# A QKV projection kernel whose first two row pairs are scheduled anew: half of the early x loads on GpSimd's queue, weight casts between evacuations, block sums in order of first use

## The chip, the cores and the metric

One core of one Trainium2 chip. The metric is the device time of one execution in microseconds (us); the profile is that of one execution, and its span leaves out a little that the time holds.

## The reference

```
def reference(x, w_qkv):              # x: 16 x 512 x 768, w_qkv: 768 x 2304, float32
    qkv = np.matmul(x, w_qkv)
    hidden = x.shape[-1]
    q, k, v = qkv[..., :hidden], qkv[..., hidden:2*hidden], qkv[..., 2*hidden:]
    return np.stack([q, k, v], axis=0).astype(np.float32)
```

So it is one product of 8192 x 768 by 768 x 2304, its result cut into three.

## The kernel before, in words

The 8192 rows of x are taken as 32 pairs of 128 rows (p = 0 to 31, `NP` is 32). The 2304 columns of the weights are two groups of 1024 (q = 0 and 1), each of two blocks of 512 (c = 0 and 1), and a remainder of 256 columns.

**A pair's way in.** `load_x` (L110) brings the 256 x 768 values into `xin` by four DMAs of 192 KB, two on SP's queue and two on ScalarE's. `transpose` (L118) is one VectorE instruction in 32 x 32 blocks, `xf<-xin`. `round_x` (L126) casts to bfloat16 on GpSimd, `xb<-xf`, and `sums_x` (L130) makes on GpSimd five blocks `s` out of `xf` (L136 to L140). `xin` has 3 buffers, `xf` 2, `xb` 4, `s` 2.

**Pairs 2 to 31** are computed by `two` (L236), with a scheme of seven half-depth products for each 256 x 1024 group (`product` and `do`, L154 and L173) on weights that were combined beforehand: `b1` (block c = 0 in bfloat16), `b22` (a rounded copy of the lower half of block c = 1) and four sums `t` (`sum_w`, L96, VectorE), which for q = 0 lie in `t_0` and for q = 1 in `t_1`. `t_1` takes the buffers of the staged q = 0 blocks (tag `tq`), so it can be written only when these have been read for the last time. Inside `two`, after the first product of each group, `early` transposes, casts and sums pair p + 1 and loads pair p + 2. The remainder (`rem`, L213) is 12 matmuls of 256 columns for each pair. A pair's first group uses q = 0 and its second q = 1.

**Pairs 0 and 1** are computed by plain matmuls (`direct`, L225: two row blocks of six matmuls of 512 columns, each evacuated on ScalarE at L234), since that needs only the weights as they arrive. The order of all this is written out by hand (L261 to L326); every engine runs its own instructions in that order and waits at the first that isn't ready. Weights land in stages: `str` (the remainder), `st` 108 and 110 (q = 0, blocks 0 and 1, 1536 KB each) and `st` 119, 121, 123, 125 (q = 1: halves h = 0 and 1 of block 0, then of block 1, 768 KB each), all on SP's queue, in between the loads of x. Block 0 of q = 0 is cast to `b1` on VectorE, the other three on ScalarE: `b1` of q = 1, and for c = 1 a buffer `bt` of which there is one.

Two places in this order are touched most. On ScalarE both casts of the next block (L280) stand behind all four evacuations of the block before. And `load_x(3)` stands at L322, behind the stores of pairs 0 and 1 on SP's queue and behind everything else on ScalarE's.

Of the kernel before, what the change touches and what calls it, by code (L numbers as in the profile page):

```python
# [9 lines left out]
def kernel(  # L10
# [20 lines left out]
    nc = tc.nc  # L31
    P = 128
    G = 32
# [4 lines left out]
    KT = K // P  # L38
# [3 lines left out]
    CB = 512  # L42
# [5 lines left out]
    bf16 = mybir.dt.bfloat16  # L48
    ident = mybir.ActivationFunctionType.Identity
# [10 lines left out]
    bt_pool = ctx.enter_context(tc.tile_pool(name="bt", bufs=1))  # L60
# [10 lines left out]
    b1 = [w_pool.tile([P, KT, CB], bf16, name=f"b1_{q}") for q in range(2)]  # L71
    b22 = [w_pool.tile([P, KH, CB], f32r, name=f"b22_{q}") for q in range(2)]
# [6 lines left out]
    def load_w(dst, j0, nj, off, cols):  # L79
        rows = w_qkv.rearrange("(p j) n -> p j n", j=KT)  # L80
        nc.sync.dma_start(dst[:], rows[:, j0:j0 + nj, off:off + cols])

    stage = {}

    def load_blocks(q, c):
        if q == 0:
            t = tq_pool.tile([P, KT, CB], fp32, name="st0", tag="tq")
            load_w(t, 0, KT, Q_OFF[q] + c * CB, CB)
            stage[q, 0, c], stage[q, 1, c] = t[:, :KH, :], t[:, KH:, :]
        else:  # L90
            for h in range(2):
                t = big_pool.tile([P, KH, CB], fp32, name="st1", tag="big")
                load_w(t, h * KH, KH, Q_OFF[q] + c * CB, CB)
                stage[q, h, c] = t[:]

    def sum_w(q, n):  # L96
        t1, t2, t3, t4 = ts[q]
        o, in0, in1 = {
            1: (t1, stage[q, 0, 1], stage[q, 0, 0]),
            2: (t2, stage[q, 1, 1], t1),  # L100
            3: (t3, stage[q, 1, 1], stage[q, 0, 1]),
            4: (t4, stage[q, 1, 0], t2),
        }[n]
        nc.vector.tensor_tensor(o, in0, in1, op=sub)

    xin, xf, xb, sr = {}, {}, {}, {}

    def load_x(p):  # L110
        t = xin_pool.tile([P, 2 * P // G, KC], fp32, name="xin")
        rows = x_flat[p * 2 * P:(p + 1) * 2 * P, :].rearrange("(g b) k -> b g k", b=G)
        for i in (0, 2, 1, 3):
            eng = nc.sync if i < 2 else nc.scalar
            eng.dma_start(t[i * G:(i + 1) * G], rows[:, :, i * KC:(i + 1) * KC])  # L115
        xin[p] = t

    def transpose(p):  # L118
        t = xf_pool.tile([P, KT, 2 * P], fp32, name="xf")
        nc.vector.transpose(  # L120
            t.rearrange("p j (g b) -> p g j b", b=G),
            xin.pop(p).rearrange("p g (a j) -> p g j a", a=G),
        )
        xf[p] = t

    def round_x(p):  # L126
        xb[p] = xb_pool.tile([P, KT, 2 * P], bf16, name="xb")
        nc.gpsimd.tensor_copy(out=xb[p][:], in_=xf[p][:])  # L128

    def sums_x(p):  # L130
        t = xf.pop(p)
        a11, a12 = t[:, :KH, :P], t[:, KH:, :P]
        a21, a22 = t[:, :KH, P:], t[:, KH:, P:]
        s = s_pool.tile([P, 5, KH, P], f32r, name="s")
        g = nc.gpsimd
        g.tensor_tensor(s[:, 1], a21, a22, op=add)  # L136
        g.tensor_tensor(s[:, 2], s[:, 1], a11, op=sub)  # L137
        g.tensor_tensor(s[:, 3], a11, a21, op=sub)  # L138
        g.tensor_copy(out=s[:, 0], in_=a22)  # L139
        g.tensor_tensor(s[:, 4], a12, s[:, 2], op=sub)  # L140
        sr[p] = s
# [28 lines left out]
    def bank():  # L170
        return ps_pool.tile([P, CB], fp32, name="ps")
# [41 lines left out]
    def rem(p):  # L213
        ps = ps_pool.tile([P, 2, REM], fp32, name="ps")
        for r in range(2):
            for j in range(KT):
                nc.tensor.matmul(  # L217
                    ps[:, r, :], xb[p][:, j, r * P:(r + 1) * P], w_rem[:, j, :],
                    start=(j == 0), stop=(j == KT - 1), skip_group_check=True,
                )  # L220
        o = or_pool.tile([P, 2, REM], fp32, name="orem")
        nc.scalar.activation(o[:], ps[:], ident)  # L222
        nc.sync.dma_start(rows_of(1, p, R_OFF - H, R_OFF - H + REM), o[:])

    def direct(p, c, o, w):  # L225

        for r in range(2):
            ps = bank()
            for j in range(KT):
                nc.tensor.matmul(  # L230
                    ps[:], xb[p][:, j, r * P:(r + 1) * P], w[:, j, :],
                    start=(j == 0), stop=(j == KT - 1),
                )
            nc.scalar.activation(o[:, r, c * CB:(c + 1) * CB], ps[:], ident)  # L234
# [24 lines left out]


    load_x(0)  # L261
    tiny = w_pool.tile([P, 1], fp32, name="tiny")
    nc.vector.memset(tiny[:], 0.0)
    nc.scalar.activation(tiny[:], tiny[:], ident)
    st_rem = big_pool.tile([P, KT, REM], fp32, name="str", tag="big")
    load_w(st_rem, 0, KT, R_OFF, REM)
    load_x(1)
    load_blocks(0, 0)
    load_blocks(0, 1)
    load_x(2)  # L270
    o0 = [quad(p, 0) for p in range(2)]
    load_blocks(1, 0)
    load_blocks(1, 1)
    o1 = [quad(p, 1) for p in range(2)]

    def cast(q, h, c, w, eng):

        dst = w[:, h * KH:(h + 1) * KH, :]
        if eng is nc.scalar:
            eng.activation(dst, stage[q, h, c], ident)  # L280
        else:
            eng.tensor_copy(out=dst, in_=stage[q, h, c])

    transpose(0)
# [8 lines left out]
    direct(0, 0, o0[0].o, b1[0])  # L293
    direct(1, 0, o0[1].o, b1[0])
    bt = bt_pool.tile([P, KT, CB], bf16, name="bt")
    for h in range(2):
        cast(0, h, 1, bt, nc.scalar)
    transpose(2)
    round_x(2)
    sums_x(2)  # L300
    direct(0, 1, o0[0].o, bt)
    store_quad(o0[0])
    direct(1, 1, o0[1].o, bt)
    store_quad(o0[1])
    sum_w(0, 1)
    sum_w(0, 2)
    nc.scalar.activation(b22[0][:], stage[0, 1, 1], ident)  # L307
    for h in range(2):
        cast(1, h, 0, b1[1], nc.scalar)
    sum_w(0, 3)  # L310
    sum_w(0, 4)
    direct(0, 0, o1[0].o, b1[1])
    direct(1, 0, o1[1].o, b1[1])
    bt = bt_pool.tile([P, KT, CB], bf16, name="bt")
    for h in range(2):
        cast(1, h, 1, bt, nc.scalar)
    direct(0, 1, o1[0].o, bt)
    store_quad(o1[0])
    direct(1, 1, o1[1].o, bt)
    store_quad(o1[1])  # L320
    nc.scalar.activation(b22[1][:], stage[1, 1, 1], ident)
    load_x(3)  # L322
    t_1 = [tq_pool.tile([P, 2, KH, CB], f32r, name=f"t_1{n}", tag="tq") for n in range(2)]
    ts[1] = [t_1[n // 2][:, n % 2] for n in range(4)]
    for n in range(1, 5):
        sum_w(1, n)  # L326

    for p in range(2, NP):
        def early():
            if p + 1 < NP:  # L330
                transpose(p + 1)
                round_x(p + 1)
                sums_x(p + 1)
            if p + 2 < NP:
# [36 lines left out]
```

## Time and profile before

| | |
|---|---|
| median of 3 runs | 398.53 us (396.7 to 399.95) |
| profiled execution, its own time | 398.28 us |
| its span in the profile | 396.5 us |
| TensorE (PE) matmul busy | 356.4 us (90%) |
| VectorE (DVE) busy | 231.6 us (58%) |
| ScalarE (ACT) busy | 185.9 us (47%) |
| GpSimd (POOL) busy | 187.0 us (47%) |
| DMA moved | 108.08 MB, mean 273 GB/s |

All times inside the execution are microseconds from the span's start. A row of the chain of waits reads: start, length, what ran. A row of the timeline reads: start, busy time, engine, line, operation, out<-in, count, and in brackets how long the engine had been idle and what released it. "q" behind an engine's name is its queue of issued DMAs. In a table by windows come busy time and count of each engine, the TensorE clock that was granted, the DMA share and GB/s.

### The profile page before, as it was taken

How to read it: one execution, taken by the hardware profiler on the slowest of the kernel's cores; microseconds unless marked ns; L12 is line 12 of the kernel's file. 1: busy time of each engine (PE TensorE's matmuls, PEld its weight loads, DVE VectorE, ACT ScalarE, POOL GpSimd, SP SyncE). 2: the span in 40 equal slices, each digit the busy share in tenths (PEclk: the TensorE clock that was granted, in tenths of full speed). 3: DMA queues.
4: the chain of work that ended last, by engine and by line, in shares of the span. 5: the costliest groups of instructions: out<-in, count | busy, mean ns of one | idle time of the engine just before them, and what ended most of it. 6: DMA issues, size and time to landing. Idle time of an engine off the chain costs nothing.

```text
span 396.5 us, 5022 instructions
## 1 busy us (share of the span) xinstructions
PE 356.4 (90%) x1709; PEld 244.5 (62%) x1740; DVE 231.6 (58%) x223; ACT 185.9 (47%) x299; POOL 187.0 (47%) x186
## 2 busy tenths in 40 slices
PE   0375796999999999999999999999999999999992
PEld 0232235666677776667666777776676666777761
DVE  2459604666555556766665655566666665555641
ACT  1246544345454454444454454544545544545540
POOL 1219301744555555454545555555445455555500
PEclk9999889899999999999999999999999999999998
DMA  8998048688888999898989889998898888989566
GB/s 210 347 328 327 32 170 201 212 253 281 298 285 281 302 292 312 288 292 265 298 283 295 289 281 290 299 311 299 282 283 281 285 288 288 288 280 310 221 240 238
DMA packets 82313, 108.08 MB, mean 273 GB/s; under 512 B 4720, under 2 KB 62832, under 8 KB 82288
## 3 DMA queue, kind: packets, MB, share of 16 engines
q1 hardware_dynamic: 64880, 95.17, 74.6%
q10 hardware_dynamic: 17408, 12.59, 10.4%
q8 instruction: 14, 0.23, 0.3%
q14 instruction: 11, 0.09, 0.1%
HBM read 32.24 MB, written 75.50 MB: 272 GB/s over the span
## 4 chain that ended last, share of the span: by engine, by line
PE 85%; DMA 5%; ACT 3%; POOL 2%; DVE 1%; issue 1%; SPq 0%; DVEq 0%; ACTq 0%
PE ps L165 69%; PE ps L217 10%; PE ps L230 6%; DMA xin<-in_x_dram 5%; DVE xf L120 1%; ACT bt L280 1%; POOL xb L128 1%; ACT b L280 1%; ACT o L234 0%; ACT b L307 0%; POOL s L137 0%; POOL s L136 0%; POOL s L138 0%; ACT orem L222 0%; SPq L115 0%
## 5 line engine op out<-in xcount | busy, mean ns | idle before, releaser
L165 PE MATMUL ps<-t,s 128*128 128x512 f32 x720 | 194.4, 412 | 0.6 <-issue 0.6
L165 PEld LDWEIGHTS ps<-t,s 128*128 128x128 f32 x720 | 133.1, 188 | 33.4 <-issue 1.1
L128 POOL CAST xb<-xf 128x1536 bf16<-128x1536 f32 x32 | 48.3, 1508 | 186.7 <-DVE xf L120 186.7
L120 DVE STREAM_TRANSPOSE xf<-xin 128x1536 f32<-128x1536 f32 x32 | 95.5, 2984 | 36.1 <-DMA xin<-in_x_dram 35.8
L165 PE MATMUL ps<-b,xb 128*128 128x512 bf16 x331 | 81.6, 380 | 2.2 <-POOL s L139 0.2
L199 DVE TENSOR_TENSOR o<-o,ps 128x512 f32<-128x512 f32 x60 | 41.3, 688 | 61.7 <-PE ps L165 61.6
L193 DVE TENSOR_TENSOR o<-o,ps 128x512 f32<-128x512 f32 x60 | 41.1, 687 | 54.9 <-ACT o L192 54.9
L217 PE MATMUL ps<-w_rem,xb 128*128 128x256 bf16 x384 | 50.0, 282 | 16.3 <-ACT w_rem L286 13.4
L179 ACT ACTIVATE o<-ps 128x512 f32<-128x512 f32 x60 | 35.7, 597 | 49.3 <-PE ps L165 47.9
L165 PEld LDWEIGHTS <-xb 128*128 128x128 bf16 x360 | 30.6, 98 | 44.9 <-issue 15.7
L192 ACT ACTIVATE o<-ps 128x512 f32<-128x512 f32 x60 | 35.9, 598 | 46.8 <-PE ps L165 46.8
L186 ACT ACTIVATE o<-ps 128x512 f32<-128x512 f32 x60 | 35.9, 599 | 44.7 <-PE ps L165 44.7
L217 PEld LDWEIGHTS <-xb 128*128 128x128 bf16 x384 | 36.1, 101 | 29.5 <-POOL xb L128 14.0
L165 PE MATMUL ps<-b,s 128*128 128x512 f32 x180 | 47.8, 402 | 3.9 <-DVE o L193 3.9
L165 PEld LDWEIGHTS ps<-b,s 128*128 128x128 f32 x180 | 34.5, 192 | 12.4 <-POOL xb L128 4.3
L183 DVE TENSOR_TENSOR o<-o,ps 128x512 f32<-128x512 f32 x60 | 37.6, 666 | 2.0 <-PE ps L165 2.0
L196 ACT ACTIVATE o<-ps 128x512 f32<-128x512 f32 x60 | 35.9, 598 | 4.9 <-PE ps L165 0.4
L222 ACT ACTIVATE orem<-ps 128x512 f32<-128x512 f32 x32 | 19.1, 598 | 32.6 <-PE ps L217 32.6
L137 POOL TENSOR_TENSOR s<-s,xf 128x384 fp32r<-128x384 f32 x30 | 31.9, 1063 | 2.3
L140 POOL TENSOR_TENSOR s<-xf,s 128x384 fp32r<-128x384 f32 x30 | 32.0, 1067 | 0.0
L136 POOL TENSOR_TENSOR s<-xf 128x384 fp32r<-128x384 f32 x30 | 31.8, 1060 | 0.0
L138 POOL TENSOR_TENSOR s<-xf 128x384 fp32r<-128x384 f32 x30 | 31.7, 1057 | 0.0
(21 smaller groups left out, 96.9 us busy)
## 6 DMA issues: line engine op xcount, KB each, us to landing
out_dram<-o SPq DMA_DIRECT2D x64, 768.0 KB, 4.3
out_dram<-o SPq DMA_DIRECT2D x64, 256.0 KB, 4.7
xin<-in_x_dram ACTq DMA_DIRECT2D x64, 192.0 KB, 5.7
xin<-in_x_dram SPq DMA_DIRECT2D x64, 192.0 KB, 6.7
out_dram<-orem SPq DMA_DIRECT2D x32, 256.0 KB, 2.3
st<-in_w_qkv_dram SPq DMA_DIRECT2D x2, 1536.0 KB, 12.0
st<-in_w_qkv_dram SPq DMA_DIRECT2D x4, 768.0 KB, 13.3
str<-in_w_qkv_dram SPq DMA_DIRECT2D x1, 768.0 KB, 10.1
```

The source lines that it names most:

```text
L120: nc.vector.transpose(t.rearrange("p j (g b) -> p g j b", b=G), xin.pop(p).rearrange("p g (a j) -> p g j a", a=G),)
L128: nc.gpsimd.tensor_copy(out=xb[p][:], in_=xf[p][:])
L140: g.tensor_tensor(s[:, 4], a12, s[:, 2], op=sub)
L165: nc.tensor.matmul(ps[:], lhs[j], rhs[j], start=(start and j == 0), stop=(j == KH - 1), skip_group_check=True,)
L179: nc.scalar.activation(c11, u.x[:], ident)
L183: nc.vector.tensor_tensor(c11, c11, u.z[:], op=add)
L186: nc.scalar.activation(c12, u.x[:], ident)
L192: nc.scalar.activation(c22, u.x[:], ident)
L193: nc.vector.tensor_tensor(c22, c22, u.y[:], op=add)
L196: nc.scalar.activation(c21, u.x[:], ident)
L199: nc.vector.tensor_tensor(c12, c12, u.y[:], op=add)
L217: nc.tensor.matmul(ps[:, r, :], xb[p][:, j, r * P:(r + 1) * P], w_rem[:, j, :], start=(j == 0), stop=(j == KT - 1), skip_group_check=True,)
```

## The change

1. Pairs 0 to 2: the two x DMAs that ScalarE issued are issued by GpSimd's queue (`gp`, software descriptor generation); from pair 4 on they stay on ScalarE.
2. `load_x(3)` moves from behind all of the direct work to right behind `transpose(0)`, half on SP, half on GpSimd.
3. `transpose(0)` is two VectorE instructions of half the size.
4. The direct work goes block by block (`block`): four groups of six matmuls with their evacuations, and a half-block's cast on ScalarE behind the second and behind the third of them.
5. On VectorE, two of q = 0's sums come ahead of `transpose(2)` and two behind it; both `b22` copies move from ScalarE to VectorE.

```diff
-    def load_x(p):
+    def load_x(p, other):
...
-            eng = nc.sync if i < 2 else nc.scalar
+            eng = nc.sync if i < 2 else other
...
-    def direct(p, c, o, w):
+    def direct(p, r, c, o, w):
...
-    load_x(0)
+    gp = nc.gpsimd
...
+    load_x(0, gp)
...
-    load_x(1)
+    load_x(1, gp)
...
-    load_x(2)
+    load_x(2, gp)
...
+    def block(q, c, w, then):
+
+        for n in range(4):
+            p, r = divmod(n, 2)
+            direct(p, r, c, (o0, o1)[q][p].o, w)
+            if c == 1 and r == 1:
+                store_quad((o0, o1)[q][p])
+            then(n)
+
+    transpose(0, 2)
+    load_x(3, gp)
     round_x(0)
     nc.scalar.activation(w_rem[:], st_rem[:], ident)
     transpose(1)
...
     for h in range(2):
         cast(0, h, 0, b1[0], nc.vector)
...
+    sum_w(0, 1)
+    sum_w(0, 2)
     transpose(2)
     round_x(2)
     sums_x(2)
...
     sum_w(0, 3)
     sum_w(0, 4)
...
+    nc.vector.tensor_copy(out=b22[0][:], in_=stage[0, 1, 1])
+    bt0 = bt_pool.tile([P, KT, CB], bf16, name="bt")
+    block(0, 0, b1[0], lambda n: n in (1, 2) and cast(0, n - 1, 1, bt0, nc.scalar))
+    block(0, 1, bt0, lambda n: n in (1, 2) and cast(1, n - 1, 0, b1[1], nc.scalar))
+    bt1 = bt_pool.tile([P, KT, CB], bf16, name="bt")
+    block(1, 0, b1[1], lambda n: n in (1, 2) and cast(1, n - 1, 1, bt1, nc.scalar))
+    block(1, 1, bt1, lambda n: None)
...
     for n in range(1, 5):
         sum_w(1, n)
+    nc.vector.tensor_copy(out=b22[1][:], in_=stage[1, 1, 1])
...
-                load_x(p + 2)
+                load_x(p + 2, nc.scalar)
```

How the change moves instructions is shown for three engines. First ScalarE from the end of the remainder's evacuations (`orem`) to pair 2's first evacuation; `st_110` is q = 0, block 1, and `st_119` to `st_125` are q = 1, `b_1_89` is `b1` of q = 1, and `b_0_90` and `b_1_91` are the `b22` copies. Before:

```order
L222 ACTIVATE orem<-ps 128x512 x2
L234 ACTIVATE o<-ps 128x512 x4
L280 ACTIVATE bt<-st_110 128x1536 x2
L234 ACTIVATE o<-ps 128x512 x4
L307 ACTIVATE b_0_90<-st_110 128x1536
L280 ACTIVATE b_1_89<-st_119 128x1536
L280 ACTIVATE b_1_89<-st_121 128x1536
L234 ACTIVATE o<-ps 128x512 x4
L280 ACTIVATE bt<-st_123 128x1536
L280 ACTIVATE bt<-st_125 128x1536
L234 ACTIVATE o<-ps 128x512 x4
L321 ACTIVATE b_1_91<-st_125 128x1536
```

And in the change, on the same engine, at the same place:

```order
L225 ACTIVATE orem<-ps 128x512 x2
L236 ACTIVATE o<-ps 128x512 x2
L283 ACTIVATE bt<-st_110 128x1536
L236 ACTIVATE o<-ps 128x512
L283 ACTIVATE bt<-st_110 128x1536
L236 ACTIVATE o<-ps 128x512 x3
L283 ACTIVATE b_1_89<-st_119 128x1536
L236 ACTIVATE o<-ps 128x512
L283 ACTIVATE b_1_89<-st_121 128x1536
L236 ACTIVATE o<-ps 128x512 x3
L283 ACTIVATE bt<-st_123 128x1536
```

Each half-block's cast now stands behind the second or the third evacuation of the block before instead of behind its fourth, and the two `b22` copies are gone from this engine.

Next GpSimd from the start of its program to the sums of pair 2 in the change. Before, its first instructions there were the three casts `xb<-xf`:

```order
L364 UNCONDITIONAL_BRANCH
L115 DMA xin<-in_x_dram 32x8x192 x8
L131 CAST xb<-xf 128x1536 x3
L139 ISA
L139 TENSOR_TENSOR s<-xf 128x384
```

Eight DMA issues now stand ahead of the first cast, the last two of them (pair 3) waiting for `transpose(0)`, whose buffer they overwrite.

Last VectorE between the casts of q = 0's block 0 (`b_0_88`) and pair 2's first addition, in the change; `t_92` is `t_0`, `t_337` and `t_338` are `t_1`:

```order
L285 CAST b_0_88<-st_108 128x1536 x2
L104 TENSOR_TENSOR t_92<-st_110,st_108 128x1536
L104 TENSOR_TENSOR t_92<-st_110,t_92 128x1536
L123 STREAM_TRANSPOSE xf<-xin 128x8x6x32
L104 TENSOR_TENSOR t_92<-st_110 128x1536
L104 TENSOR_TENSOR t_92<-st_108,t_92 128x1536
L313 CAST b_0_90<-st_110 128x1536
L104 TENSOR_TENSOR t_337<-st_123,st_119 128x1536
L104 TENSOR_TENSOR t_337<-st_125,t_337 128x1536
L104 TENSOR_TENSOR t_338<-st_125,st_123 128x1536
L104 TENSOR_TENSOR t_338<-st_121,t_337 128x1536
L324 CAST b_1_91<-st_125 128x1536
```

Before, the transpose of pair 2 stood ahead of all eight sums, and no copy to `b22` stood here; the sums themselves are the same.

More of the change, by code (lines that the diff above doesn't have):

```diff
@@ L113, in load_x, with transpose @@
         for i in (0, 2, 1, 3):
-            eng = nc.sync if i < 2 else nc.scalar
+            eng = nc.sync if i < 2 else other
             eng.dma_start(t[i * G:(i + 1) * G], rows[:, :, i * KC:(i + 1) * KC])
         xin[p] = t
-    def transpose(p):
+    def transpose(p, pieces=1):
         t = xf_pool.tile([P, KT, 2 * P], fp32, name="xf")
[L120 to L123, printed above, removed]
+        src = xin.pop(p)
+        n = 2 * P // G // pieces
+        for c in range(pieces):
+            nc.vector.transpose(
+                t[:, :, c * n * G:(c + 1) * n * G].rearrange("p j (g b) -> p g j b", b=G),
+                src[:, c * n:(c + 1) * n].rearrange("p g (a j) -> p g j a", a=G),
+            )
         xf[p] = t
@@ L223, in rem @@
         nc.sync.dma_start(rows_of(1, p, R_OFF - H, R_OFF - H + REM), o[:])
-    def direct(p, c, o, w):
[L227 to L234, printed above, removed]
+    def direct(p, r, c, o, w):
+        ps = bank()
+        for j in range(KT):
+            nc.tensor.matmul(
+                ps[:], xb[p][:, j, r * P:(r + 1) * P], w[:, j, :],
+                start=(j == 0), stop=(j == KT - 1),
+            )
+        nc.scalar.activation(o[:, r, c * CB:(c + 1) * CB], ps[:], ident)
     def two(a, b, fill, early, mid):
@@ L282, in cast @@
             eng.tensor_copy(out=dst, in_=stage[q, h, c])
-    transpose(0)
+    def block(q, c, w, then):
[7 more added lines that the diff above has]
+    load_x(3, gp)
     round_x(0)
@@ L292 @@
         cast(0, h, 0, b1[0], nc.vector)
[L293 to L297, printed above, removed]
+    sum_w(0, 1)
+    sum_w(0, 2)
     transpose(2)
@@ L300 @@
     sums_x(2)
[L301 to L309, printed above, removed]
     sum_w(0, 3)
     sum_w(0, 4)
[L312 to L322, printed above, removed]
+    nc.vector.tensor_copy(out=b22[0][:], in_=stage[0, 1, 1])
[5 more added lines that the diff above has]
+    block(1, 1, bt1, lambda n: None)
     t_1 = [tq_pool.tile([P, 2, KH, CB], f32r, name=f"t_1{n}", tag="tq") for n in range(2)]
```

## The prediction, made before the change was run

> **What bounds the kernel now.** I read the table by windows first, to see which stretch isn't at its limit.
>
> ```profile
> core 0: us, PE busy (x) PEld busy (x) DVE busy (x) ACT busy (x) POOL busy (x), PEclk, DMA share, GB/s
> 0.00:10.00 10.00, 0.00 (x0) 0.00 (x0) 2.95 (x2) 1.49 (x2) 1.18 (x5) 1.00 0.85 210
> 10.00:20.00 10.00, 3.67 (x17) 2.43 (x18) 4.54 (x3) 2.08 (x2) 1.96 (x2) 1.00 1.07 348
> 20.00:30.00 10.00, 7.89 (x35) 3.79 (x35) 5.07 (x3) 5.21 (x7) 1.41 (x1) 1.00 1.07 329
> 40.00:50.00 10.00, 7.27 (x25) 2.87 (x26) 6.59 (x4) 5.14 (x7) 3.33 (x2) 0.84 0.08 28
> 100.00:150.00 50.00, 49.65 (x248) 35.40 (x252) 30.11 (x33) 24.58 (x42) 27.75 (x30) 1.00 0.90 289
> ```
>
> From 100 us on PE is busy 49.65 of 50 us: nothing in this change shortens that. Up to 30 us DMA is full; at 40 to 50 us it stands at 28 GB/s while PE has gaps. So only the first 73 us can give anything, and the chain of waits says what they are made of:
>
> ```profile
> 4.23 10.29 DMA xin<-in_x_dram
> 14.55 2.92 DVE xf L120
> 17.52 1.48 POOL xb L128
> 19.05 2.74 PE ps L217 x12
> 21.79 5.37 PE ps L230 x24
> ...
> 27.78 2.75 ACT bt L280 x2
> ...
> 30.57 4.71 PE ps L230 x21
> ...
> 35.90 1.37 ACT b L307
> 37.27 2.75 ACT b L280 x2
> ...
> 40.06 5.89 PE ps L230 x21
> ...
> 46.47 2.86 ACT bt L280 x2
> ...
> 50.17 5.55 PE ps L230 x19
> ...
> 57.33 7.71 DMA xin<-in_x_dram
> 65.12 2.96 DVE xf L120
> 68.14 1.46 POOL xb L128
> ...
> 73.13 7.44 PE ps L165 x32
> 80.57 1.33 PE ps L217 x12
> ...
> 84.06 7.39 PE ps L165 x32
> ```
>
> Three kinds of loss stand there: four pieces in which PE waits for ScalarE's casts (27.78, 35.90, 37.27, 46.47), the load of pair 3 that begins at 57.33, and the start, bound by landing data. Pair 3 starts at 73.13, pair 4 at 84.06: a well-fed pair takes 10.93 us.
>
> **The change part by part.** Rows for the prices:
>
> ```profile
> 1.76 0.91 ACTq L115 DMA_DIRECT2D xin<-in_x_dram  x2
> 6.07 2.90 DVE L120 STREAM_TRANSPOSE xf<-xin 128x1536 f32<-128x1536 f32 x1 [5.20 <-DMA xin<-in_x_dram]
> 18.37 2.30 DVE L282 CAST b<-st 128x1536 bf16<-128x1536 f32 x2 [0.91 <-DMA st<-in_w_qkv_dram]
> 23.30 0.60 ACT L234 ACTIVATE o<-ps 128x512 f32<-128x512 f32 x1 [0.87 <-PE ps L230]
> 24.59 0.60 ACT L234 ACTIVATE o<-ps 128x512 f32<-128x512 f32 x1 [0.70 <-PE ps L230]
> 55.55 2.11 PE L165 MATMUL ps<-b,xb 128*128 128x512 bf16 x9
> ```
>
> *Where the direct work starts.* It needs b1 of q = 0 and the end of `rem(1)`. Ahead of that block's last byte must land x0, str and x1 (768 KB each), the block (1536 KB), and GpSimd's halves of x2 and x3 (384 KB each): 4608 KB or 4.72 MB. The first ten microseconds moved 2.10 MB, the rest at 348 GB/s takes 7.5 us: landed at 17.5, cast (2.30) by 19.8. For x1, 2.36 MB with x2's half 2.75 MB give 11.9; it landed at 14.5 before; I take the middle, 13.2. Then transpose 2.92, cast 1.48 and rem(1) 2.74 give 20.4, the later of the two. It was 21.79: **-1.4 us**. `transpose(0)` in two halves does the same elements and adds one instruction at 6 to 9 us, when DVE has nothing else: nothing.
>
> *GpSimd's issues.* No row shows this queue issuing. Nearest:
>
> ```profile
> L115 ACTq DMA_DIRECT2D xin<-in_x_dram x64: 317/414/1297, 0.7 to 357.7; - x64
> L115 SPq DMA_DIRECT2D xin<-in_x_dram x64: 312/1212/1850, 0.7 to 360.6; - x64
> DMA to landing us min/median/max: 3.2/6.3/12.3
> ```
>
> Low end 0.41 us each (ScalarE's median), high end 6.3 (it holds GpSimd until the data have landed). I take SP's median, 1.2, since the other two queues issue the same transfer in that order of size. Eight issues stand ahead of the cast of pair 0, the last two behind `transpose(0)`, which ended at 9.0: GpSimd is free at the later of 9.0 + 2d and 0.8 + 8d, that is 11.4. The casts then end at 12.9 and, with x1, at 17.6; rem(0) (12.9 to 15.6) is over before rem(1) can begin: covered. The cover ends when GpSimd is free later than 13.4 (13.4 + 1.5 + 2 x 2.74 = 20.4), at d = 1.6; beyond it every 0.1 us costs 0.8 us. The remainder's weights stand no further back on SP's queue than before. SP's order is unchanged but for x3, now behind the weights and ahead of the stores; a store of pairs 0 and 1 that goes a little later holds up nobody, since their buffers are not taken again before pair 3.
>
> *Blocks and casts.* A group of six matmuls takes 1.29 (24.59 - 23.30), a block 5.17; the first evacuation comes 1.51 after the block's start (23.30 - 21.79) and takes 0.60; a cast takes 1.38 (2.75 / 2). ScalarE from a block's start: evacuations to 2.11 and 3.40, cast 3.40 to 4.78, evacuation to 5.38, cast to 6.76, evacuation to 7.36. The next block begins at 5.17 on the first half, runs three matmuls (0.65), and waits from 5.82 to 6.80 for the second half: 0.98 lost at each of three borders. So 3 x 6.15 + 5.17 = 23.6 us, from 20.4 to 44.0. Before it was 21.79 to 55.55, 33.76 us: **-10.2 us**. ScalarE's loss of the two `b22` copies is in this.
>
> *Pair 2.* Its products took 55.55 to 73.13, 17.58 us, since pair 3's x came so late. Now x3 is asked for some 40 us earlier, ahead of the stores, and pair 2 takes 10.93: **-6.65 us**, if DVE keeps up. DVE's rows:
>
> ```profile
> 28.46 1.71 DVE L104 TENSOR_TENSOR t<-st,st 128x1536 fp32r<-128x1536 f32 x1
> 28.59 2.90 POOL L128 CAST xb<-xf 128x1536 bf16<-128x1536 f32 x1 [9.60 <-DVE xf L120]
> 30.20 2.90 DVE L104 TENSOR_TENSOR t<-st,t 128x1536 fp32r<-128x1536 f32 x1
> 42.41 2.55 DVE L104 TENSOR_TENSOR t<-st,st 128x1536 fp32r<-128x1536 f32 x1
> 67.99 1.25 DVE L183 TENSOR_TENSOR o<-o,ps 128x512 f32<-128x512 f32 x2
> PE ps L165 <- DVE o L193: 3.9, 1, 3.9
> ```
>
> A sum costs 1.71 with GpSimd quiet, 2.55 beside it (both engines' instructions are longer there: the cast `xb` 2.90 against 1.48). Block 1 of q = 0 lands 1.57 MB after block 0, at 329 to 348 GB/s 4.5 us: 22.0. Two sums to 25.4, transpose of pair 2 to 28.4, two sums to 33.5, the copy to `b22`, four sums (10.2) and the other copy, transpose of pair 3. For a copy on DVE I have bounds of 1.15 (half the L282 row) and 2.55; I take 1.5. That gives 35.0, 45.2, 46.7 and 49.6. Pair 3's cast follows to 51.1; PE wants it at 44.0 + 10.93 = 54.9. The tighter one: pair 2's third product (do 3, block a) waits for DVE's L193 addition, as the last row shows for pair 2 before. That addition comes behind the transpose and two L183: 49.6 + 1.25 + 0.64 = 51.5. The product stands 9.5 into a pair (7.44 + 1.33 and one more product): 53.5. Slack **2.0 us**; nothing is charged.
>
> *The clock.* Of two equal pieces of 21 matmuls in the chain, one took 4.71 (at 30.57) and one 5.89 (at 40.06, window clock 0.84), so a cold start costs 1.2 us. The gaps of 0.98 are shorter than those before 40.06 and 50.17, but PE also pauses before and after rem(1). I charge half of one: **+0.6 us**. The Trainium skill, page TensorE: Matmul & The Clock Gate, section Part 1: The HAM clock gate, says that the clock is halved after an idle window of about 3.4 us and given back after a busy one of that length; by it the gaps of 0.98 would cost nothing and the sum would be 0.6 less. The trace agrees in part: a long gap came before 40.06, a piece without that loss before 30.57.
>
> *Sum.* -1.4 - 10.2 - 6.65 + 0.6 = -17.6 us. The profiled execution took 398.28 us (span 396.5), so 380.7; that execution lies 0.25 under the median of the runs, so **380.9 us**.
>
> **Rivals.**
>
> *GpSimd issues slowly, and the kernel ends slower (chance 0.05).* The eight issues hold up the cast of pair 0 and so every matmul. From d = 1.6 it costs; the direct work starts at GpSimd's free time + 7.0. At d = 4.5, between the trace's shortest way to landing (3.2) and its median (6.3), GpSimd is free at 36.8, the work starts at 43.8 instead of 20.4: 23.4 us, 404.3. It passes the time before from d = 3.8. For it: software makes the descriptors, 256 rows of 768 bytes for each DMA, and no row shows its speed. Against: the other queues need 0.3 to 1.9 us. A milder form, d from 1.6 to 3.8 (chance 0.10), gives at 2.5 a free time of 20.8, a start at 27.8 and 388.3. The Trainium skill, page SBUF — State Buffer, section A bandwidth-pool intuition that's wrong, reports such a DMA at 0.62 us alone and 3.1 us beside a VectorE copy. Here DVE's first cast ran at 18.37, after all eight issues by my sum; with 3.1 each the time would be some 12 us above my forecast.
>
> *DVE becomes the bound of pair 2 (0.07).* DVE now has two more copies and ends its list with pair 3's transpose. With all ten sums and copies at the longest row, 2.90: 22.0 + 29.0 + 2.93 + 2.96 + 1.89 = 58.8 for the addition, 5.3 behind the product's 53.5: 386.2. For it: the slack is 2.0 us alone. Against: the sums behind the first two ran at 2.55 or less.
>
> *The casts are in the way (0.08).* ScalarE runs in order: if st 110 lands after 23.8 (20.4 + 3.4), evacuations queue behind a cast that waits for data, and interleaving doesn't do what it says. Landed at 27.0 (before, the cast at 27.78 found it there), the casts end at 28.4 and 30.4, the second block's first group at 31.05 instead of 27.85: 3.2 us, 384.1. For it: DMA is full until 30 us and x3 adds 768 KB. Against: only half of x3 goes ahead of this block.
>
> **How the numbers follow.** Forecast 0.70, DVE 0.07, casts 0.08, GpSimd mild 0.10, GpSimd slow 0.05. The likeliest gives 380.9. Low end: no cold start, direct work at 19.8, copies at 1.15 for DVE with slack unchanged: 379.7, and runs of one kernel lie 1.8 below their median, 377.9; I give 377, since x1 at 11.9 instead of 13.2 would let `rem(1)` end earlier still. High end: 388.5, which takes in the DVE and cast cases and about half of the mild GpSimd one; left out are some 0.15. Faster by over 1% (below 394.5; 1% is about what a measurement of this kernel can tell from no change): forecast, DVE, casts and 0.07 of the mild case, to d = 3.3: 0.92. Within 1%: 0.03. Slower: 0.05.
>
> **What would show it.** Right: the first direct matmul at about 20.4; ScalarE's casts between evacuations, with PE gaps near 1 us at three borders instead of 3 to 5; pair 2 from 44 to 55, with no wait for `xin`; pair 3's start near 55 instead of 73.13 and 10.9 us a pair from there on. GpSimd's eight issues over by about 11.4, each near 1.2. Wrong: rem(0) waiting for `xb` beyond 14.9 (issues slow), ScalarE idle for DMA `st` ahead of a cast (weights late), PE waiting for DVE's addition in pair 2 (DVE late), or a pair from 3 on longer than 10.9.

## The result, and the profile after

The changed kernel takes **383.81 us** (median of 4 runs, 383.2 to 384.69); the kernel before, on the same chip, 398.61 us (396.7 to 399.95). The ratio is 0.9634, with a 95% interval of 0.9589 to 0.9678. The forecast was 380.9 us, in a range of 377.0 to 388.5. So the direction and the range hold, and the saving is 14.8 us where 17.6 was forecast.

The profiled execution took 383.2 us, its span is 381.4. It is cut below at three points that both profiles show: the first matmul of the direct work, the first product of pair 2 and the first of pair 3. The column "forecast" holds the terms of the prediction's sum; its charge for a cold clock stands with the blocks.

| stage | before | after | change | forecast |
|---|---|---|---|---|
| up to the direct work's first matmul | 21.58 | 23.31 | +1.73 | -1.4 |
| direct blocks, to pair 2 | 33.97 | 24.07 | -9.90 | -9.6 |
| pair 2, to pair 3 | 17.58 | 11.08 | -6.50 | -6.65 |
| pair 3 to the end | 323.37 | 322.94 | -0.43 | 0 |
| span | 396.5 | 381.4 | -15.1 | -17.65 |

Three of the four stages came out within 0.5 us of their forecast. The start went the other way, by 3.1 us. The table by windows of the changed kernel shows both the gain and that loss (columns as before: PE, PEld, DVE, ACT and POOL busy, granted clock, DMA share, GB/s):

```profile
0.00:10.00 10.00, 0.00 (x0) 0.00 (x0) 0.19 (x2) 1.49 (x2) 3.82 (x10) 1.00 0.87 189
10.00:20.00 10.00, 2.74 (x12) 1.64 (x12) 5.73 (x3) 2.08 (x2) 3.38 (x4) 1.00 1.06 271
20.00:30.00 10.00, 9.17 (x38) 4.59 (x40) 5.02 (x4) 4.27 (x6) 0.72 (x1) 1.00 1.06 316
...
40.00:50.00 10.00, 9.27 (x43) 4.27 (x41) 9.96 (x6) 6.87 (x10) 7.21 (x4) 1.00 0.84 314
100.00:150.00 50.00, 49.65 (x242) 34.84 (x246) 32.59 (x33) 25.00 (x42) 24.95 (x26) 1.00 0.89 282
```

From 40 to 50 us PE is busy 9.27 of 10 us where it was 7.27, the clock is 1.00 where it was 0.84, and DMA moves 314 GB/s where it moved 28. From 100 us on nothing has changed. But in the first 20 us DMA, as full as before by its share, moves 189 and 271 GB/s where it moved 210 and 348. The chain of waits of the changed kernel shows what the time up to pair 3 is made of now:

```profile
2.37 0.63 SPq L115
...
3.04 13.11 DMA xin<-in_x_dram
16.27 2.93 DVE xf L123
19.25 1.48 POOL xb L131
20.78 2.74 PE ps L220 x12
23.52 3.39 PE ps L232 x12
27.52 1.37 ACT bt L283
28.90 0.49 ACT o L236
29.39 1.38 ACT bt L283
...
58.46 7.39 PE ps L168 x32
```

ScalarE's casts alternate with its evacuations (27.52, 28.90, 29.39), the load of pair 3 is no longer in the chain, and pair 3 starts at 58.46. The load of pair 1's x is what got worse: it lands 1.6 us later than before, and the row ahead of it names its queue, SP's, not GpSimd's. The timeline of the changed kernel has the start, the borders and pair 2 (start, busy, what, and in brackets the idle time before it):

```profile
1.32 3.61 POOL L115 DMA_DIRECT2D xin<-in_x_dram  x6 [0.87 <-POOLq L353]
9.87 2.94 DVE L123 STREAM_TRANSPOSE xf<-xin 128x768 f32<-128x768 f32 x2 [9.00 <-DMA xin<-in_x_dram]
13.11 1.16 POOL L115 DMA_DIRECT2D xin<-in_x_dram  x2 [8.18 <-DVE xf L123]
21.98 1.83 DVE L285 CAST b<-st 128x1536 bf16<-128x1536 f32 x2 [2.79 <-DMA st<-in_w_qkv_dram]
23.31 6.17 PE L232 MATMUL ps<-b,xb 128*128 128x512 bf16 x24
30.81 4.69 PE L232 MATMUL ps<-bt,xb 128*128 128x512 bf16 x21 [0.68 <-ACT bt L283]
36.83 4.69 PE L232 MATMUL ps<-b,xb 128*128 128x512 bf16 x21 [0.68 <-ACT b L283]
47.38 2.11 PE L168 MATMUL ps<-b,xb 128*128 128x512 bf16 x9
49.62 3.05 DVE L123 STREAM_TRANSPOSE xf<-xin 128x1536 f32<-128x1536 f32 x1
53.75 0.68 DVE L196 TENSOR_TENSOR o<-o,ps 128x512 f32<-128x512 f32 x1
56.84 1.55 PE L168 MATMUL ps<-b,s 128*128 128x512 f32 x6
```

Six of GpSimd's issues take 3.61 us together and the other two 1.16: near 0.6 each. Even so, the data land later. Pair 0's x is there at 9.87 (before, the transpose began at 6.07), and the cast of the first block begins at 21.98, 2.79 us after VectorE had become idle (before, at 18.37).

### The profile page after: what moved, and what is told of

It reads as the page before. It is cut to its first block, busy times and chain, and to the rows that moved or that the text cites. A ratio compares the mean times of both kernels' runs of the same rounds, so it can differ in the third digit from the quotient of the medians.

```text
span 381.4 us, 5036 instructions
## 1 busy us (share of the span) xinstructions
PE 351.8 (92%) x1709; PEld 243.1 (64%) x1740; DVE 233.4 (61%) x226; ACT 182.9 (48%) x297; POOL 191.2 (50%) x194
## 3 DMA queue, kind: packets, MB, share of 16 engines
q0 software_dynamic: 512, 1.57, 1.8%
## 4 chain that ended last, share of the span: by engine, by line
PE 89%; DMA 3%; ACT 3%; issue 1%; DVE 1%; SPq 1%; POOL 0%; DVEq 0%; ACTq 0%
PE ps L168 75%; PE ps L220 11%; DMA xin<-in_x_dram 3%; PE ps L232 3%; ACT bt L283 1%; DVE xf L123 1%; ACT b L283 1%; ACT o L236 1%; POOL xb L131 0%; SPq L115 0%; SPq L81 0%; ACT orem L225 0%; DVEq L123 0%; ACTq L225 0%
## 5 line engine op out<-in xcount | busy, mean ns | idle before, releaser
L123 DVE STREAM_TRANSPOSE xf<-xin 128x1536 f32<-128x1536 f32 (+1 forms) x33 | 95.9, 2909 | 13.9 <-DMA xin<-in_x_dram 13.9
L220 PEld LDWEIGHTS <-xb 128*128 128x128 bf16 x384 | 36.0, 101 | 31.4 <-POOL xb L131 18.5
L168 PE MATMUL ps<-b,s 128*128 128x512 f32 x180 | 46.5, 393 | 0.0
L140 POOL TENSOR_TENSOR s<-s,xf 128x384 fp32r<-128x384 f32 x30 | 31.1, 1038 | 2.3
```

The costliest lines, as they stand in the source:

```text
L123: nc.vector.transpose(t[:, :, c * n * G:(c + 1) * n * G].rearrange("p j (g b) -> p g j b", b=G), src[:, c * n:(c + 1) * n].rearrange("p g ...
L168: nc.tensor.matmul(ps[:], lhs[j], rhs[j], start=(start and j == 0), stop=(j == KH - 1), skip_group_check=True,)
L220: nc.tensor.matmul(ps[:, r, :], xb[p][:, j, r * P:(r + 1) * P], w_rem[:, j, :], start=(j == 0), stop=(j == KT - 1), skip_group_check=True,)
```

## The experiments

Two theories about the start were put to the chip first. Theory A: the kind of queue is at fault. With a part of x on GpSimd's queue the data of the first 20 us move more slowly, and the rest of the change is worth what was forecast. Theory B: the prediction counted the bytes or their order wrongly, and any queue would start as late. Each time below is a median; the ratio is against the kernel before on the same chip.

**The change with ScalarE's queue in place of GpSimd's.** Against the changed kernel:

```diff
-    gp = nc.gpsimd
+    gp = nc.scalar
+    load_x(0, gp)
     tiny = w_pool.tile([P, 1], fp32, name="tiny")
...
-    load_x(0, gp)
```

> The changed kernel with GpSimd's eight early x loads on ScalarE's queue instead (pairs 0 to 3, and pair 0's ahead of ScalarE's first instructions, as before the change); all else as changed. Theory A (the software queue makes the early loads slow: 189 and 271 GB/s in the first two stretches of ten microseconds against 210 and 348): x0 lands near 6 instead of 9.9, the first direct matmul comes at 20.5 to 21.8 instead of 23.3, and the time falls from 383.8 to 381.2 to 382.5. Theory B (what came later is pair 3's load and the deeper line of weights on SP's queue, whichever engine issues the other halves): the first direct matmul stays at 23 or later and the time at 383.8 within 0.6.

Measured: 379.94 us (379.32 to 380.31), ratio 0.9547 (0.9509 to 0.9585), so 3.9 us less than the change, and 2.8 less than the change when it ran again (382.7, on another chip, see below). That is more than theory A expected (381.2 to 382.5). The timeline of this kernel:

```profile
12.89 2.93 DVE L123 STREAM_TRANSPOSE xf<-xin 128x1536 f32<-128x1536 f32 x1 [3.86 <-DMA xin<-in_x_dram]
17.57 1.83 DVE L285 CAST b<-st 128x1536 bf16<-128x1536 f32 x2 [1.75 <-DMA st<-in_w_qkv_dram]
...
19.88 5.34 PE L232 MATMUL ps<-b,xb 128*128 128x512 bf16 x24
43.15 2.10 PE L168 MATMUL ps<-b,xb 128*128 128x512 bf16 x9
54.24 1.89 PE L168 MATMUL ps<-b,xb 128*128 128x512 bf16 x8
```

The prediction had x1 at 13.2, the first block at 17.5, the direct work at 20.4, pair 2 at 44.0 and pair 3 at 54.9. On ScalarE's queue they come at 12.89, 17.57, 19.88, 43.15 and 54.24. At 17.57 DMA had moved 4.71 MB, where the prediction counted 4.72. So its count of bytes was right, and so was the rate it used, for a start without GpSimd's queue. Theory B falls. Not all of the 3.9 us is the queue's: the first block takes 5.34 us here and 6.17 in the change, and that is the clock's doing, as the next section shows.

**The kernel before with GpSimd's queue alone** for pairs 0 to 2, nothing else changed:

```diff
-            eng = nc.sync if i < 2 else nc.scalar
+            eng = nc.sync if i < 2 else (other or nc.scalar)
...
+    gp = nc.gpsimd
+    load_x(0, gp)
...
-    load_x(1)
+    load_x(1, gp)
...
-    load_x(2)
+    load_x(2, gp)
```

> The kernel before, with one part of the change: the six early x loads that ScalarE issued (pairs 0 to 2) are issued on GpSimd's queue; pair 3's load stays where it was. Theory A: x0 lands near 9.5, the first direct matmul comes at 22.8 to 24 instead of 21.6, all behind it moves as much, and the time rises from 398.6 to 399.8 to 401. Theory B: the start stays within 0.4 us and the time within 0.5.

Measured: 401.71 us (399.13 to 404.05, 10 runs), ratio 1.0072 (1.004 to 1.0104). This part of the change costs time, somewhat more than the 399.8 to 401 of theory A. The timeline of this kernel:

```profile
16.11 2.91 DVE L120 STREAM_TRANSPOSE xf<-xin 128x1536 f32<-128x1536 f32 x1 [3.35 <-DMA xin<-in_x_dram]
...
23.15 5.42 PE L230 MATMUL ps<-b,xb 128*128 128x512 bf16 x24
```

x1 lands 1.56 us later than before (16.11 against 14.55) and the direct work begins 1.57 later (23.15 against 21.58), nearly the +1.73 of the whole change. The profiled execution is 1.4 us longer than that of before, the medians lie 3.3 apart, and these runs spread more widely than those of any other kernel here. Where the rest of the 3.3 arises was not settled.

**`load_x(3)` early, alone,** in the kernel before (its second half on ScalarE's queue):

```diff
     transpose(0)
+    load_x(3)
...
-    load_x(3)
```

> The kernel before, with one part of the change: pair 3's x is asked for right behind the transpose of pair 0 (SP and ScalarE), not behind the direct work. The prediction's sum: pair 2 takes 10.9 instead of 17.6 us, and x3's 384 KB on ScalarE's queue put off q = 0's first block by up to 1.1 us: 392 to 393.1. Theory B: its early bytes put off the start by the whole 1.5 us that the changed kernel lost: 393.5. Rival (pair 2 waits for VectorE's sums instead): more than 394.5.

Measured: 391.36 us (390.41 to 392.52), ratio 0.9834 (0.9783 to 0.9885). The chain of waits has no wait for x3 any more:

```profile
54.90 1.94 PE ps L165 x9
...
66.73 7.39 PE ps L165 x32
```

Pair 2 takes 11.99 us here instead of 17.58, with one gap left at 56.84. The direct work began 2.57 us earlier in this execution (19.01), where the sum expected it up to 1.1 later, and so the time is under the expected 392. Of the 2.57 us 0.81 was left at pair 2 (54.74). The waits for ScalarE's casts are as long as before (3.41 us in both kernels from the end of the first block to the 21 matmuls of the second); what is lost is the pace behind them. The 21 matmuls at 27.78 take 6.39 us at a granted clock of 0.73, where the same 21 took 4.71 at 1.00 before, and those at 38.96 take 6.15 instead of 5.89.

**Blocks, casts and sums alone,** without the queue and without the early x3 (parts 4 and 5 of the change). Against the changed kernel, beside the three loads without `gp` and the whole transpose:

```diff
-    transpose(0, 2)
-    load_x(3, gp)
+    transpose(0)
...
     block(1, 1, bt1, lambda n: None)
+    load_x(3)
```

> The kernel before, with parts 4 and 5 of the change alone: the direct work block by block with the casts between the evacuations, the sums in the new order and both copies on VectorE; the early loads on SP and ScalarE and pair 3's load late, as before. The prediction's sum: the direct work takes 23.6 to 24.1 instead of 33.8 us, pair 2 still some 17.6: 388.4 to 389. Rival (the casts were hidden behind loads that land no sooner): the gaps before the casts' matmuls stay over 2 us and the time above 392.

Measured: 387.77 us (387.13 to 389.06), ratio 0.9749 (0.9708 to 0.9791). The chain of waits:

```profile
47.21 7.98 DMA xin<-in_x_dram
...
63.22 8.17 PE ps L165 x32
```

The direct work took 24.76 us (20.67 to 45.43) where it took 33.97. The wait for x3 has moved forward with it and kept its size: pair 2 still takes 17.79. The three parts by themselves make +3.28, -7.07 and -10.66, together -14.45 us; all of them together made -14.8, and -16.2 when the change ran again (382.7 against 398.94). So the parts nearly add up, and neither of the two gains hides the other. The transpose in two halves was not run by itself.

**The change again, and the sums in another order.** The second kernel differs from the change in this:

```diff
-    sum_w(0, 1)
-    sum_w(0, 2)
     transpose(2)
     round_x(2)
     sums_x(2)
+    sum_w(0, 1)
+    sum_w(0, 2)
```

> The changed kernel itself, beside the next three on one chip. All theories: 383.8 within 0.8, the first direct matmul near 23.3, pair 3 near 58.5.

> The changed kernel with one part of it undone: the transpose of pair 2 stands ahead of all sums on VectorE again, as before the change. Theory A (VectorE has about 2 us of slack in pair 2: its addition ended at 54.4, the product behind it began near 56.3): pair 3's transpose and the additions move back by 1 to 3 us, the time by 0 to 1.2 us, to 383.8 to 385. Theory B (VectorE's order is what lets pair 2 run without a gap): PE waits for VectorE in pair 2 for more than 2 us and the time is above 386.

Measured: the change 382.7 us (382.16 to 384.07), ratio 0.9596 (0.9562 to 0.963); with the sums behind, 383.13 us (382.64 to 385.34), ratio 0.9622 (0.9582 to 0.9662). The repeated change is 1.1 us under its first median, a little outside the 0.8 that was expected. The runs do not tell the two kernels apart. The timeline with the sums behind has a wait in pair 2 that the change doesn't have:

```profile
52.75 2.59 PE L168 MATMUL ps<-t,s 128*128 128x512 f32 x10 [1.14 <-ACT o L182]
```

The evacuation that PE waits for here had itself waited 2.46 us for VectorE's sums. So in this execution their order costs 1.1 us, as theory A has it; the medians lie 0.4 apart, and whether the order is worth anything over several runs stays open. In the repeated change block 1 of q = 0 landed later: VectorE waited 4.38 us for it, as this row of its timeline shows. ScalarE's cast of it began at the same 28.30, only 0.06 us after the evacuation ahead of it, so that the first border grew by 0.17 us (0.85 instead of 0.68).

```profile
28.30 1.76 DVE L104 TENSOR_TENSOR t<-st,st 128x1536 fp32r<-128x1536 f32 x1 [4.38 <-DMA st<-in_w_qkv_dram]
```

**One queue alone.** A third theory, C, was that a second queue of any kind is what hurts or helps. Against the change:

```diff
-    gp = nc.gpsimd
+    gp = nc.sync
```

> The changed kernel with all sixteen early x loads (pairs 0 to 3) on SP's queue alone, in its order of issue; no other queue loads. Theory A (the software queue itself is slow; one hardware queue moves 768-byte rows at about 0.2 MB/us, 2 KB rows at 0.385): ahead of q = 0's first block stand 3.93 MB, 2.36 of them at 0.2 to 0.22, so it lands near 17 to 18.5, x1 near 13.5, the direct work starts at 20 to 21.5, and the time is 380 to 381.5, below 383.8. Theory C (what helps is a second queue that runs beside SP's, of whatever kind): x1 and the weights land as late as in the changed kernel or later (16.3 and 22.0), and the time is 383.5 or more.

Measured: 380.4 us (379.63 to 381.14), ratio 0.9543 (0.9512 to 0.9574), the same as with ScalarE's queue. Theory C falls: what matters is whether GpSimd's queue is among them. The timeline of this kernel:

```profile
16.58 2.24 DVE L285 CAST b<-st 128x1536 bf16<-128x1536 f32 x2 [0.96 <-DMA st<-in_w_qkv_dram]
18.95 6.60 PE L232 MATMUL ps<-b,xb 128*128 128x512 bf16 x24
```

The block lands 1 us earlier than on ScalarE's queue, but its 24 matmuls take 6.60 instead of 5.34, at a granted clock of 0.81.

**How many transfers, or how early?** Two kernels split GpSimd's share: pair 0 on ScalarE and pairs 1 to 3 on GpSimd, and pairs 0 and 1 on GpSimd and pairs 2 and 3 on ScalarE. Theory A1: a start with GpSimd's queue costs by the bytes that it carries ahead of the first block. Theory A2: it costs by its late first transfer, pair 0's.

```diff
     gp = nc.gpsimd
+    load_x(0, nc.scalar)
...
-    load_x(0, gp)
```

> The changed kernel with pair 0's two loads on ScalarE's queue (issued first, as before the change) and those of pairs 1 to 3 on GpSimd's: six software-queue loads instead of eight. Theory A1 (each byte on the software queue costs DMA time): q = 0's first block lands three quarters of the way from 17.6 (all on ScalarE) to 22.0 (all on GpSimd), near 20.9, and the time is 382 to 383. Theory A2 (only the software queue's late beginning counts, which x0 feels): with x0 near 6.1 the rest is as on ScalarE's queue, block 1 lands near 18 and the time is 380 to 381.

```diff
-    load_x(2, gp)
+    load_x(2, nc.scalar)
...
-    load_x(3, gp)
+    load_x(3, nc.scalar)
```

> The changed kernel with pairs 0 and 1 on GpSimd's queue as changed and pairs 2 and 3 on ScalarE's: four software-queue loads instead of eight. Theory A1: q = 0's first block lands about half way, near 19.8, and the time is 381.3 to 382.3. Theory A2: x0 lands as late as in the changed kernel (9.5 to 9.9), and the time stays at 383 to 384.

Measured: 383.05 us (382.21 to 384.09), ratio 0.9608 (0.9566 to 0.9651), and 383.28 us (382.11 to 383.42), ratio 0.9606 (0.9568 to 0.9645). The timeline of the first:

```profile
6.31 2.95 DVE L123 STREAM_TRANSPOSE xf<-xin 128x768 f32<-128x768 f32 x2 [5.44 <-DMA xin<-in_x_dram]
...
21.40 1.83 DVE L285 CAST b<-st 128x1536 bf16<-128x1536 f32 x2 [2.70 <-DMA st<-in_w_qkv_dram]
```

Pair 0 lands 3.6 us earlier than in the change, and the first block only 0.6: A2 falls, and A1's 20.9 is missed by 0.5. The timeline of the second:

```profile
20.08 1.83 DVE L285 CAST b<-st 128x1536 bf16<-128x1536 f32 x2 [1.63 <-DMA st<-in_w_qkv_dram]
...
29.40 6.38 PE L232 MATMUL ps<-bt,xb 128*128 128x512 bf16 x21 [1.05 <-ACT bt L283]
```

The block lands near A1's 19.8. The time of the whole kernel is above what A1 gave and within A2's 383 to 384, but not for A2's reason. The next block landed late, so that PE waited for its cast (0.84 and 1.05 us), and behind that wait the granted clock was 0.50 from 29.94 to 33.35: the second block's 21 matmuls took 6.38 instead of 4.69. So A1 holds for the landing and misses the end.

**The remainder of pair 1 at the first border.** With queues that work (pairs 0 and 1 on ScalarE, 2 and 3 on SP), `rem(1)` no longer stands ahead of the first block:

```diff
     rem(0)
-    rem(1)
...
     block(0, 0, b1[0], lambda n: n in (1, 2) and cast(0, n - 1, 1, bt0, nc.scalar))
+    rem(1)
```

> A version built on the readings: x of pairs 0 and 1 on SP and ScalarE, all four loads of pairs 2 and 3 on SP behind the weights they would hold up, and the remainder of pair 1 between the first and the second direct block instead of ahead of the first. Theory A: 3.93 MB ahead of q = 0's first block land it near 15.4, the direct work starts at about 16.7 instead of 23.3, the remainder covers one border's wait, and pair 2 starts near 41 instead of 47.4: 377 to 378.5. Rival (the loads of x1 or block 1 of q = 0 are now what is late, and the pauses only move): 379.5 or more.

Measured: 380.55 us (379.88 to 382.31), ratio 0.9553 (0.9516 to 0.9591): the expected gain did not come. PE's timeline:

```profile
12.22 2.71 PE L220 MATMUL ps<-w_rem,xb 128*128 128x256 bf16 x12 [12.22 <-ACT w_rem L299]
18.15 7.11 PE L232 MATMUL ps<-b,xb 128*128 128x512 bf16 x24 [3.22 <-DVE b L285]
25.11 1.47 PE L220 MATMUL ps<-w_rem,xb 128*128 128x256 bf16 x12
```

The block begins 1.73 earlier than with ScalarE's queue alone (18.15 against 19.88), after 3.22 us of idle PE, and takes 1.77 longer (7.11 against 5.34). The row for the block in the table by windows shows the granted clock, 0.76; in the kernel with ScalarE's queue it is 1.00 over the block (19.88 to 25.20).

```profile
18.15:25.20 7.05, 7.03 (x25) 2.81 (x25) 4.69 (x4) 3.08 (x5) 0.00 (x0) 0.76 1.09 295
```

So the lead was lost to the clock: it was at 0.50 from 18.79 to 22.20. That the missing remainder brought this about is not shown, for the next kernel keeps it and its block runs as slowly. A remainder takes 1.47 behind the block, at the full clock, and 2.71 ahead of it.

**The same queues with the remainder where it was** (pairs 0 and 1 on ScalarE, 2 and 3 on SP):

```diff
-    gp = nc.gpsimd
+    gp = nc.scalar
...
-    load_x(2, gp)
+    load_x(2, nc.sync)
...
-    load_x(3, gp)
+    load_x(3, nc.sync)
```

> A version: pairs 0 and 1 on SP and ScalarE, all four loads of pairs 2 and 3 on SP behind the first weights, the remainders ahead of the direct work as in the change (they warm the clock while PE waits anyway). q = 0's first block lands near 16.7, as in the version with the remainder at the border; the direct work starts at 19 to 19.5 with the clock up for most of it: 379 to 380, 0.5 to 1 below that version. Rival (pair 1's x is the bound of the start, not the weights): no difference to all on ScalarE, 380 within 0.5.

Measured: 380.36 us (379.62 to 381.22), ratio 0.9541 (0.9495 to 0.9587), no difference to ScalarE's queue for all four, as the rival said. Again the first block runs long (at a granted clock of 0.78), as PE's timeline shows:

```profile
19.42 6.83 PE L232 MATMUL ps<-b,xb 128*128 128x512 bf16 x24
```

Against the kernel with the remainder at the border, which has the same queues, this block begins 1.27 us later and takes 0.28 less; pair 2 begins at 44.14 here and at 43.63 there. So moving the remainder is worth 0.5 us in these two executions and nothing that the medians show. The four changed kernels without GpSimd's queue, at 379.94 to 380.55, are not told apart by their runs. Each beats both the kernel before and the changed one (383.81 and 382.7).

## Why the prediction was right where it was, and where it failed

*Where the direct work starts* is the step that failed. The prediction had pair 1's x at 13.2, the start 7.2 behind it and "-1.4 us"; it was +1.73. The x came at 16.27, 3.1 later, and that is the whole miss, since in the chain of waits the start hangs on it. The first block, "landed at 17.5, cast (2.30) by 19.8", was 4.5 late too. The prediction took the bytes at 210 and then 348 GB/s, the rates of a start in which ScalarE and SP issued. The rate differs with the queues in use. These rows of the tables by windows are for 2 to 13 us, in which DMA is full in every kernel. The kernel before:

```profile
2.00:13.00 11.00, 0.00 (x0) 0.10 (x1) 2.90 (x1) 2.36 (x3) 1.46 (x1) 1.00 1.07 266
```

The kernel before with GpSimd's queue alone:

```profile
2.00:13.00 11.00, 0.00 (x0) 0.00 (x0) 2.90 (x1) 1.36 (x3) 3.10 (x7) 1.00 1.06 227
```

The change:

```profile
2.00:13.00 11.00, 0.00 (x0) 0.00 (x0) 2.94 (x2) 0.22 (x2) 2.93 (x6) 1.00 1.06 230
```

The change with ScalarE's queue:

```profile
2.00:13.00 11.00, 0.00 (x0) 0.11 (x1) 3.06 (x3) 1.19 (x2) 1.46 (x1) 1.00 1.07 280
```

At one DMA share, 1.06 to 1.07, 266 and 280 GB/s move without GpSimd's queue and 227 and 230 with it. The other kernels fall on the same two sides, at 253 to 282 without it and 220 to 247 with it, but not far apart: the 247 is the change itself, when it ran again. The landing parts them too: pair 1's x is there at 12.70 to 14.55 in the seven kernels without GpSimd's queue and at 15.53 to 17.00 in the six executions with it. The kernel before is the latest of its side. In the change's own rates the sum comes out so: 1.89 MB in the first 10 us, and the remaining 2.83 of 4.72 MB at 271 GB/s in 10.4, so landed at 20.4. It landed at 21.98. By then 1.89 + 2.71 + 0.63 (1.98 us at 316) = 5.2 MB had moved, so that some 0.5 MB of other transfers went ahead of the block's last byte, which the prediction's order doesn't have. They belong to block 1, the next on SP's own queue: that queue had moved 3.68 MB by then, where its halves of x, `str` and the first block are 3.15. The slower rate thus explains 2.9 of the 4.5 us, and the order the rest. In the repeated change, with 202 and 282 GB/s, the same sum gives 2.1 of 4.6 to the rate and more to the order, so the landing repeats (22.10) and its split doesn't. Pair 1's x is alike: up to the half of x2 2.75 MB stand ahead of it, 13.2 at the change's rates, and 3.40 MB had moved when it came.

Which transfers are late can be read from the tables of queues for 2 to 13 us (packets, MB, share of the 16 engines' time). q1 is SP's queue, q0 GpSimd's and q10 ScalarE's. The first two rows are the change, the other two the change with ScalarE's queue:

```profile
q1 hardware_dynamic: 1575, 1.36, 57.8%
q0 software_dynamic: 375, 1.17, 48.2%
...
q1 hardware_dynamic: 2009, 1.90, 65.3%
q10 hardware_dynamic: 1628, 1.18, 42.1%
```

GpSimd's queue moves as much as ScalarE's does in its place, 1.17 MB against 1.18; it is SP's queue that moves 1.36 MB instead of 1.90. For a us of packet time a DMA engine moves 13.8 KB on GpSimd's queue (1.17 MB / (0.482 x 16 x 11 us)) and 13.4 on SP's beside it, against 15.9 and 16.5 in the other kernel. So in this stretch GpSimd's transfers are not the slow ones: both queues are slower, and the bytes that go missing are SP's, those of the row that bounds the start among them. Why that is so was not shown. The packets differ, with 3.1 KB on average on GpSimd's queue against 0.7 on ScalarE's; whether their size holds up SP's was not tested.

The Trainium skill speaks to this. Its page DMA: Bandwidth & Descriptors, section Issuing engine by pattern, gives simple loads and stores to SyncE, and calls the queues of SyncE and ScalarE generally faster than GpSimd's. The runs agree: 379.94 and 380.4 against 383.81. Its section Rules for kernel authors says that spreading transfers over SP, ScalarE and GpSimd doesn't help bandwidth. Between SP and ScalarE the runs agree (380.4 with one, 379.94 with two); with GpSimd it was worse than no help, 220 to 247 GB/s instead of 253 to 282.

*GpSimd's issues.* The prediction took 1.2 us each; the trace shows 0.58 (583 ns at least, 586 in the median, 723 at most). The cover that it named held: the last two issues waited 8.18 us for the transpose of pair 0, were over at 14.27, and the cast of pair 0 behind them was done in time for x1, which landed at 16.27. The first sign of being wrong, `rem(0)` waiting for `xb` beyond 14.9, did come (15.79), but from pair 0's late x and not from slow issues. So the rival "GpSimd issues slowly" named the right engine, yet the cost came in the data and not in the issue.

*Blocks and casts.* Right in mechanism and size. The blocks follow each other at 6.02 us (36.83 - 30.81) where 6.15 was forecast, so a border costs 0.85 instead of 0.98 over the 5.17 of a bare block; 0.68 of it is the wait that the rows show. All four blocks took 24.07, that is 20.68 bare, 2.55 for three borders and 0.84 left, and this lies in the first block: its first 12 matmuls take 3.39 in the chain (at 23.52), where half a bare block is 2.59. The table by windows prints a clock of 1.00 there, but the trace's records of the granted clock only begin at 24.97, with the full clock, and the table prints 1.00 ahead of them too. The pace shows in the weight loads (PEld), of which each matmul has one:

```profile
24.59 0.15 PEld L232 LDWEIGHTS <-xb 128*128 128x128 bf16 x1 [0.28 <-issue]
25.00 4.85 PEld L232 LDWEIGHTS <-xb 128*128 128x128 bf16 x23 [0.26 <-issue]
```

Up to 25.00 one comes every 0.43 us, behind it 23 in 4.85, so one in 0.21. From 23.31 to 24.97 the block thus ran at half pace, which costs 0.83, all that was left. So the charge of 0.6 for *the clock* was right in kind and somewhat small. Its reason, the pauses around `rem(1)`, was near: no pause took the clock away here, TensorE had not been granted it yet, and both remainders ran at half pace too (2.74 us each, against 1.48 for pair 2's at 54.82). The gaps at the borders cost nothing beyond themselves: the 21 matmuls behind each take 4.69 at a granted clock of 1.00. The Trainium skill's rule that the prediction weighed (TensorE: Matmul & The Clock Gate, Part 1: The HAM clock gate), by which so short a gap costs nothing, agrees with these 4.69.

*Pair 2.* Right: 11.08 us where 10.93 was forecast, and x3 no longer bounds it. VectorE was the nearer danger, and the slack is as computed: pair 3's transpose ended at 52.67 (forecast 49.6, with a start 2.9 us earlier), the addition at 54.43, and the product behind it began at 56.84, a slack of 2.4 where 2.0 was forecast. The copies to `b22`, put at 1.5, took 1.75 beside GpSimd and 0.95 without it. That the rival "DVE becomes the bound" did not come follows from this row. The rival "the casts are in the way" came in part in the kernel with pairs 0 and 1 on GpSimd, where late weights held up ScalarE's first cast by 1.26 us; in the change itself it did not.

*The sum.* The start is off by 3.1 us, the other terms together by -0.6 (-0.3 in the blocks, +0.15 in pair 2, -0.43 in the rest): 2.5 for the profiled execution (383.2 against 380.7) and 2.9 for the medians. The change is worth 14.8 us in spite of its first part; without that part it is worth 18.5 (398.43 - 379.94, on one chip). That the range held is in part luck: its high end of 388.5 was set for slow issues, a late VectorE and late casts, and none of these is what came.

## What to carry to other kernels

Where a start is bound by landing data, a change of queue is priced by the rate at which the data then arrive, not by the time its issues take: here the issues cost half of what was assumed and the start came 3 us later than forecast, on bytes of the queue that was not changed. On an engine that works in order, a cast for the next block goes between the evacuations of this one, and the load that a later stage waits for is asked for before the stores: these two gains add up, as running each by itself showed (-10.7 and -7.1 us). And a lead at the start is not yet a gain: where TensorE's full clock comes later than the work, part of the lead is lost again at half pace, so look at the pace of the matmuls there, and not only at the printed clock.

## What the runs showed that was not expected

- With a part of x on GpSimd's queue, DMA at nearly the same busy share (1.04 to 1.08) moved 220 to 247 GB/s from 2 to 13 us, against 253 to 282 without it. Moving pair 0 off that queue, or pairs 2 and 3, did not bring the time back (383.05 and 383.28 us).
- The direct work's first block of 24 matmuls took 5.34 us where the two remainders ahead of it ran back to back or 0.85 us apart (three kernels), from 5.42 to 6.92 where they ran 2.2 to 3.5 us apart, and 7.11 with one alone. The pause's length by itself doesn't decide it (5.56 before, with a pause of 2.97). What does is when the full clock is granted: in all thirteen profiles the time above 5.34 is, within 0.07 us, half of what the block ran without it. The first record is at 22.01 before (block at 21.58: 0.22 expected, 0.22 measured), at 26.32 in the repeated change (23.41: 1.46 and 1.45), at 19.82 with ScalarE's queue (19.88: none and none). In four kernels the clock was granted early, while `rem(0)` ran or just behind it, and halved again for 3.41 us over the block, as from 19.00 to 22.41 in the kernel with ScalarE's and SP's queues (block at 19.42: 1.50 and 1.49). In the three kernels without GpSimd's queue that began this block 0.5 to 1.7 us earlier than the one with ScalarE's queue, that lead was lost again in the block.
- An engine's copy beside another's: a `b22` copy on VectorE took 0.95 us with GpSimd quiet and 1.75 while GpSimd ran; a sum 1.76 quiet, and 2.05 to 3.03 while GpSimd ran. In the one pair that can be followed the one that began first kept its pace: a sum at 33.09 took 1.73, GpSimd's cast at 33.24 took 2.90 instead of 1.47, and the sum behind, at 34.73, took 3.03.
